# One bias table over the whole score row, transposed probabilities in two PSUM banks, an early query weight, later keys, and the projection's sums on VectorE

## The chip, the cores and the metric

The kernel runs on one core of a Trainium2 chip. A core has five engines, each with its own queue of instructions worked off in order: TensorE (PE, matrix products; its weight loads are listed apart as PEld), VectorE (DVE), ScalarE (ACT), GpSimd (POOL) and SyncE (SP), which here only issues transfers (DMA). SBUF is the core's working memory and PSUM, eight banks of 512 four-byte words on each of 128 partitions, is where PE writes. An engine waits for another, or for a transfer, at a semaphore; while it waits, everything behind in its queue waits too.

The metric is the device time of one execution in microseconds (us). Single executions scatter by about 0.3%.

## The reference

A two-layer trunk for a prompt of 1024 frames and eight sample streams of 16 frames. Layer 0 is RWKV-7 time mixing, layer 1 is banded attention; each is followed by a gated feed-forward part. All numbers are float32. The change lies in the attention of layer 1, which is this (cut to what matters; 16 heads of 64, chunks of 64 frames, eight past chunks):

```python
q_pos = pos0 + start + jnp.arange(qb)
k_pos = pos0 + start - hist_len + jnp.arange(band)
rel = jnp.clip(q_pos[:, None] - k_pos[None, :], -REL_CLIP, REL_CLIP) + REL_CLIP
bias = rel_table[:, rel].astype(jnp.float32)
allowed = ((k_pos[None, :] >= 0) & (k_chunk[None, :] <= q_chunk[:, None])
           & (k_chunk[None, :] >= q_chunk[:, None] - N_PAST_CHUNKS))
s = jnp.einsum('bqhd,bkhd->bhqk', q_b, k_b).astype(jnp.float32) * scale + bias[None]
s = jnp.where(allowed[None, None], s, NEG_INF)
p = jax.nn.softmax(s, axis=-1)
return jnp.einsum('bhqk,bkhd->bqhd', p.astype(v_b.dtype), v_b)
```

The bias depends on the distance of query and key, clipped at 128 frames: over all keys further back it is one constant for each head, and a constant drops out of a softmax. The output is then multiplied by `wb_o` (the projection), gated and added to the stream.

## The kernel before, in words

float32 products are made from two rounded halves (`split`: ACT makes the high half, DVE the difference), three products each.

Attention goes over eight **pairs** of heads (`pair(n)`, L1736), and in a pair over 16 **tiles** (`tile`, L1784): eight blocks of 128 queries for each of the two heads, e = 0 and 1. A tile has up to 640 keys: `nn` near ones (128 or 256), whose bias varies, and `nf` far ones (up to 384), whose bias is the constant. In the eight pairs 64 tiles have 640 keys, 16 have 512, 16 have 384, 16 have 256 and 16 have 128. What the kernel keeps is the negated score, so that the largest score is a minimum.

A tile goes in stages, and `advance` (L1767) interleaves them with those of the tiles before and with other work:

- PE writes the scores into `S` (two banks wide, two buffers). For blocks 4 to 7 an additional matmul of `m1r`, a constant set up at L1638 to L1643, adds 1e30 to the first 64 far keys for the second 64 queries.
- DVE takes the minimum of the far part (`tensor_reduce`, L1809), then one pass over the near part adds the table `bt` and takes the minimum of that and of the far one (L1810; it shows in the profile as a custom instruction and a second one that reads its accumulator).
- ACT takes the exponential with the sum (L1811), DVE normalizes (L1813, L1814).
- PE transposes the probabilities `P` in blocks of 128 into `PT`, a PSUM space of two banks in one buffer (L1819), ACT copies them to `pts` (L1820), and PE multiplies them with the values `vf` into `O`.

The **table** of a head comes from `prep` (L126), which lays the bias values out on the host: 128 queries by 256 keys. At a pair's start `pair` loads it into `bw` (one buffer), DVE subtracts the constant and negates into `bt` (four buffers, L1748), and POOL writes the mask's corner (L1749). `samples` (L1850) does the like for the sample streams with `sbw` and `sbt`, eight small loads a pair; a sample's probabilities, its product with the cached values `vc` and the result's transposition use `PT` too (L1894, the products under the helper's line L139, L1909), and DVE copies the result into `so` (L1913).

Beside the tiles runs a generator, `qgen`: the **queries** for pair n+2 (`queries`, L1722: the weight `wq[n]` is loaded in two halves `h`, split into `wh` and `wl`, and multiplied into `acc`; then a norm, `ht` and `xin`), and in the last two pairs part of the projection. `kprep` and `qprep` load the keys and queries of one head from DRAM into a `slot` and split them (names `h` in the profile). For the even head of the next pair they are called at a pair's start, for the odd one near its end. `kv` (up to L1605) makes keys and values, and the queries of pairs 0 and 1, ahead of the first pair.

`attproj` (L1920) does the rest of the projection for the second half of the frames, and between its steps `strassen_in` (L1280) prepares the feed-forward input: norms, and sums and differences of blocks (L1295), which run on POOL unless another engine is given.

The order on each engine is not written out: a scheduler goes through the program as it is written, with its own idea of durations, and places each instruction in its engine's queue. A buffer's next use waits until all that read its former content have ended; pools of several buffers go round.

Of the kernel before, what the change touches and what calls it, by code (L numbers as in the profile page):

```python
# [9 lines left out]
F32R = mybir.dt.float32r  # L10
# [66 lines left out]
def prep(i):  # L77
    i = {k: np.asarray(v) for k, v in i.items()}
    d = {}
# [43 lines left out]
    d["ck"] = i["cache_k"].reshape(8, 512, 8, 128).transpose(2, 3, 0, 1)  # L123
    d["cv"] = i["cache_v"].reshape(8, 4, 128, 8, 128).transpose(3, 2, 0, 1, 4)
    q, u = np.arange(128)[:, None], np.arange(256)[None, :]
    d["rel"] = i["rel_bias"][0][:, np.minimum(256 + q - u, 256)]  # L126
    for l in range(2):
        d[f"wg{l}"] = _tiles(i["w_gate"][l])
        d[f"wu{l}"] = _tiles(i["w_up"][l])
# [12 lines left out]
class Trunk:  # L142
# [1419 lines left out]
    def kv(self, H, X, end):  # L1562
        nc = self.nc
        kn, qn = (self.cp.tile([128, 1], F32, name=n) for n in ("kn2", "qn2"))
        nc.vector.tensor_scalar(kn, self.P("kn", 0), -0.5, None, ALU.mult)
        nc.vector.tensor_scalar(qn, self.P("qn", 0), 0.5 * 0.125, None, ALU.mult)
        self.qn = qn
        nw = 4
        W = [self.halves(self.a["wk"][n]) for n in range(nw)]
        for c in (1, 0):  # L1570
            for n in range(nw):
                self.head(n, c, W[n], H, kn[:, 0:1], self.kT)
                for _ in range(3):
                    next(end, None)
            for _ in end:
                pass
        for n in range(nw, 8):
            W = self.halves(self.a["wk"][n])
            for c in (1, 0):
                self.head(n, c, W, H, kn[:, 0:1], self.kT)  # L1580
        self.HQ = {}
        Aq = self.gain("nm1", 56)
        for n in range(4):
            W = [h for u in range(2) for h in self.halves(self.a["wv"][n, u])]
            for c in range(2):
                for w in range((4, 5)[c]):
                    ws = slice(w * 128, (w + 1) * 128)
                    pz = self.wide()[:, 0:256]
                    for k in range(8):
                        ks = slice(k % 2 * 256, (k % 2 + 1) * 256)  # L1590
                        wh, wl = W[k // 2]
                        self.mm3(pz, H[c][0][k][:, ws], H[c][1][k][:, ws], wh[:, ks], wl[:, ks], k == 0, k == 7)
                    vt = self.ev("vt")[:, 0:256]
                    nc.scalar.activation(vt, pz, AF.Copy)
                    nc.sync.dma_start(self.o["v"][4 * c + w, :, n * 256:(n + 1) * 256], vt)
                if n == 3:
                    self.HQ[c] = self.feats(c, F32R), self.feats(c, F32R)
                    for _ in self.normed_split(c, *X[c], Aq, 48, *self.HQ[c]):
                        pass
        self.KQ = {}  # L1600
        for e in range(2):
            self.kprep(0, e)
        for n in range(2):
            if n:
                self.evt = lambda tag: self.slot(1)  # L1605
            W = self.halves(self.a["wq"][n])
            for c in range(2):
                self.head(n, c, W, self.HQ, qn[:, 0:1], self.qT)
            if n == 0:
                for e in range(2):  # L1610
                    self.qprep(0, e)
# [18 lines left out]
    def attention(self, ctx):  # L1630
# [4 lines left out]
        self.evt = lambda tag: self.pp.tile([128, 320], F32, tag=tag, name=self.nm(tag), bufs={"xin": 2, "ht": 5}[tag])  # L1635
        self.qbd = at.tile([128, 4, 2, 16], F32, name="qbd")
        nc.gpsimd.memset(self.qbd, 0.0)
        m1 = self.att("pts", [128, 640], 2)[:, 0:192]  # L1638
        self.m1r = at.tile([128, 192], F32R, name="m1r")
        nc.gpsimd.memset(m1, 0.0)  # L1640
        nc.gpsimd.memset(m1[0:1, 64:128], 1.0)
        nc.gpsimd.memset(m1[0:1, 128:192], 1e30)
        nc.scalar.activation(self.m1r, m1, AF.Copy)  # L1643
        self.X, self.xs = {}, {}
        self.O = self.bank("O", 1)
        self.flow = [None] * 3
        for n in range(8):
            if n < 6:
# [73 lines left out]
    def queries(self, n):  # L1722

        nc = self.nc
        W = self.halves(self.a["wq"][n])
        yield
        for c, o, m in ((0, 0, 256), (0, 256, 256), (1, 0, 320), (1, 320, 320)):
            yield from self.head_steps(n, c, o, m, W, self.HQ, self.qn[:, 0:1], self.qT)
# [6 lines left out]

    def pair(self, n):  # L1736
        nc = self.nc
        if n < 7:
            self.kprep(n + 1, 0)
            self.qprep(n + 1, 0)  # L1740
        vf = self.att("vf", [128, 8, 128], 2)
        nc.sync.dma_start(vf, self.o["v"][0:8, :, n * 128:(n + 1) * 128].rearrange("w p d -> p w d"))
        bias = []
        for e in range(2):
            r = self.att("bw", [128, 256], 1)
            nc.sync.dma_start(r, self.a["rel"][2 * n + e])
            bt = self.att("bt", [128, 256], 4)
            nc.vector.tensor_scalar(bt, r, r[:, 0:1], -1.0, ALU.subtract, ALU.mult)  # L1748
            nc.gpsimd.memset(bt[0:64, 192:256], 1e30)  # L1749
            bias.append(bt)  # L1750
        order = [(e, qt) for qt in range(8) for e in range(2)]
        groups = self.samples(n)
        for i, (e, qt) in enumerate(order):
            self.advance(self.tile(n, qt, e, vf, bias[e]))
            if n == 6 and i in (4, 5, 6, 8, 9, 10):
                self.xprep(*divmod((4, 5, 6, 8, 9, 10).index(i), 3))
                if i == (4, 5, 6, 8, 9, 10)[2]:
                    self.qgen = self.proj_part()
            if n == 7 and i in (4, 5):
                self.xprep(i - 4, 3)  # L1760
            if (e, qt) == (0, 7) and n < 7:
                self.kprep(n + 1, 1)
                self.qprep(n + 1, 1)
            if i in (1, 9):
                self.advance(next(groups))
# [16 lines left out]
    def tile(self, n, qt, e, vf, bias):  # L1782
# [7 lines left out]
        h = slice(64 * e, 64 * e + 64)  # L1790
        kq = self.KQ[n, e]

        def score(ps, t0, m, mask=False):
            ks = slice(t0 * 128, t0 * 128 + m)
            mm(nc, ps, kq[0][:, qsl], kq[1][:, ks], True, False)
            if mask:
                mm(nc, ps[:, 0:64], self.m1r[:, 0:128], self.m1r[:, 128:192], False, False)
            mm(nc, ps, kq[0][:, qsl], kq[2][:, ks], False, True)


# [1 line left out]
        P = self.att("P", [128, 640], 3)  # L1802
        S = self.wide_bank("S", 2)
        if nf:
            score(S[:, 512 - nf:512], k0, nf, qt >= 4)
        near = S[:, 512:512 + nn]
        score(near, n0, nn)
        if nf:
            nc.vector.tensor_reduce(st[:, 0:1], S[:, 512 - nf:512], AX.X, ALU.min)  # L1809
        nc.vector.tensor_tensor_reduce(near, near, bias[:, 256 - nn:256], 1.0, st[:, 0:1] if nf else 3.0e38, ALU.add, ALU.min, st[:, 1:2])  # L1810
        nc.scalar.activation(P[:, 0:nf + nn], S[:, 512 - nf:512 + nn], AF.Exp, bias=st[:, 1:2], scale=-1.0, accum_out=st[:, 2:3])  # L1811
        yield
        nc.vector.reciprocal(st[:, 4:5], st[:, 2:3])  # L1813
        nc.vector.tensor_scalar(P[:, 0:nf + nn], P[:, 0:nf + nn], st[:, 4:5], None, ALU.mult)  # L1814
        yield
        pts = self.att("pts", [128, 640], 2)
        pt = self.wide_bank("PT", 1)
        for j in range(nk):
            nc.tensor.transpose(pt[:, j * 128:(j + 1) * 128], P[:, j * 128:(j + 1) * 128], self.C("ident"))  # L1819
        nc.scalar.activation(pts[:, 0:nk * 128], pt[:, 0:nk * 128], AF.Copy)  # L1820
        yield
        if not e:
            self.even = pts
# [11 lines left out]
    def heads_out(self, n, t0, O):  # L1835
# [1 line left out]
        nc = self.nc  # L1837
        w = O.shape[-1]
        if n < 7:
            o = self.att("o", [128, 256], 2)  # L1840
            nc.vector.tensor_copy(o[:, 0:w], O)
            nc.sync.dma_start(self.og[n, :, t0:t0 + w], o[:, 0:w])
            return
# [4 lines left out]
    def samples(self, n):  # L1848
        nc = self.nc
        qs, kn = self.att("qsm", [128, 128]), self.att("ksm", [128, 128])  # L1850
        for t, src in ((qs, self.qT), (kn, self.kT)):
            nc.sync.dma_start(t, src[:, n, 1024:1152])
        r = self.att("sbw", [128, 144], 1)
        for e in range(2):
            for b in range(4):
                nc.sync.dma_start(r[b * 32 + e * 16:b * 32 + e * 16 + 16], self.a["rel"][2 * n + e, 0:16, 0:144])
        bt = self.att("sbt", [128, 144], 1)
        nc.vector.tensor_scalar(bt, r, r[:, 0:1], -1.0, ALU.subtract, ALU.mult)
        so = self.att("so", [128, 8, 16], 2)
        for g in range(2):  # L1860
            yield self.sample_group(n, g, qs, kn, bt, so)
# [1 line left out]
    def sample_group(self, n, g, qs, kn, bt, so):  # L1863
# [25 lines left out]
        nc.vector.reciprocal(st[:, 4:5], st[:, 2:3])  # L1889
        yield  # L1890
        pts = self.att("pts", [128, 640], 2)
        pt = self.wide_bank("PT", 1)
        for j in range(4):
            nc.tensor.transpose(pt[:, j * 128:(j + 1) * 128], P[:, j * 128:(j + 1) * 128], self.C("ident"))  # L1894
        nc.tensor.transpose(pt[0:16, 512:640], P[:, 512:528], self.C("ident"))
        nc.scalar.activation(pts[:, 0:512], pt[:, 0:512], AF.Copy)
        nc.scalar.activation(pts[0:16, 512:640], pt[0:16, 512:640], AF.Copy)
        yield
        O = self.wide_bank("PT", 1)
        quarters = [(b, slice(b * 32, b * 32 + 32)) for b in range(4)]  # L1900
        for j in range(4):
            for b, bs in quarters:
                mm(nc, O[bs, 0:128], pts[:, j * 128 + b * 32:j * 128 + b * 32 + 32], vc[:, b, j], j == 0, False)
        for b, bs in quarters:
            mm(nc, O[bs, 0:128], pts[0:16, 512 + b * 32:512 + b * 32 + 32], vn[:, b], False, True)
        on = self.att("on", [128, 128], 1)
        nc.vector.tensor_scalar(on, O[:, 0:128], st[:, 4:5], None, ALU.mult)
        pt = self.wide_bank("PT", 1)
        nc.tensor.transpose(pt[:, 0:128], on, self.C("ident"))  # L1909
        pv = pt[:, 0:128].rearrange("p (b e t) -> p b e t", b=4, e=2)  # L1910
        for e in range(2):
# [5 lines left out]
    def attproj(self, B, x2, x3, rest):  # L1917
# [5 lines left out]
        A = self.gain("nf1", 80)  # L1923
        r = self.sq_done(next(rest))
        t = [self.slot(1)[:, :1024] for _ in range(4)]
        sub = self.strassen_in(B, x3, r, A, 72, 0, [t[k // 2][:, k % 2 * 512:(k % 2 + 1) * 512] for k in range(8)])
        st = self.sq_open()
        st.acc = self.rs[:, 640:1280]
        for n in range(8):
# [63 lines left out]
```

## Time and profile before

| | |
|---|---|
| runs timed | 3: 3821.11, 3823.53 and 3833.7 us |
| median | 3823.53 us |
| the profiled execution's own time | 3810.6 us |
| its span, first to last instruction | 3808.8 us |
| clock granted to TensorE, mean | 0.944 |
| the attention's pairs, about | 2430 to 2900 us of the span |
| the rest of the projection and the feed-forward input, about | 2900 to 3000 us |

The profile is one execution. In its rows a group has its line, engine, operation, what it writes and reads, its count, then busy us and the mean ns of one, then the idle time of the engine just before with what ended it. Rows of waits have the engine and line that waited, the engine and line that it waited for, us in all, times, and the longest. Rows of a timeline begin with the time of start and the duration in us. PE's matmuls are pipelined, so that the duration of one is longer than the distance between two; busy time over count is nearer to what one costs.

### The profile page before, as it was taken

Reading aid. Unit: us, or ns where it says so; the run is one execution under the profiler, and the core shown is the slowest. Engines: PE = TensorE matmul, PEld = TensorE weight load, DVE = VectorE, ACT = ScalarE, POOL = GpSimd, SP = SyncE. Lnnn points to the kernel's source line nnn. Section 1 sums busy time; section 2 is a strip of 40 time slices with the busy share of each in tenths; the row PEclk is TensorE's granted clock in tenths of the full one; section 3 lists DMA queues with packets and bytes.
Section 4 is the critical chain, followed back from the end, with each engine's and each line's share of the span. In section 5 each row is a group of like instructions: output and inputs, shape, how many; then the busy total and the mean of one; then the engine's idle time right before and its main releaser. Section 6 shows DMA issues by size and latency. Waiting matters only on the chain.

```text
span 3808.8 us, 72340 instructions
## 1 busy us (share of the span) xinstructions
PE 3494.9 (92%) x28614; PEld 3089.7 (81%) x28614; DVE 2282.6 (60%) x4484; ACT 1574.8 (41%) x3007; POOL 589.1 (15%) x516
## 2 busy tenths in 40 slices
PE   5789989989899799999999899789889799999999
PEld 3677778777667699999888879677677699999998
DVE  4666667765445855455456742666675755545667
ACT  5545546554223533333311353565654533333310
POOL 0000000000011154443000100000000245544000
PEclk8887899899699899999999999999999899999999
DMA  5776776676665322224655112454564322222521
GB/s 209 235 221 168 206 221 178 194 211 199 189 193 176 124 81 75 76 74 145 221 177 182 69 67 95 148 157 130 156 202 162 113 87 73 76 75 95 172 86 66
DMA packets 426995, 550.87 MB, mean 145 GB/s; under 512 B 128384, under 2 KB 294784, under 8 KB 422176
## 3 DMA queue, kind: packets, MB, share of 16 engines
q1 hardware_dynamic: 351344, 447.53, 36.9%
q0 software_dynamic: 22224, 80.36, 7.0%
q10 hardware_dynamic: 53088, 18.36, 2.1%
q8 instruction: 225, 3.69, 0.4%
q14 instruction: 114, 0.93, 0.1%
HBM read 412.70 MB, written 133.40 MB: 143 GB/s over the span
## 4 chain that ended last, share of the span: by engine, by line
PE 67%; DMA 12%; DVE 10%; ACT 5%; issue 4%; SPq 1%; ACTq 0%; POOL 0%; DVEq 0%; POOLq 0%
PE S L139 32%; PE PT L139 16%; PE acc L139 10%; PE st L139 3%; PE O L139 2%; PE G L139 1%; PE PT L1819 1%; PE aux L139 1%; DVE h L269 1%; DMA TT<-Z 1%; DVE wlo L269 1%; PE Y L139 1%; ACT pts L1820 1%; DMA raw<-in_rw_o 1%; DMA Z<-T 0%
## 5 line engine op out<-in xcount | busy, mean ns | idle before, releaser
L139 PE MATMUL S<-h,w 128*128 128x320 f32 (+1 forms) x4944 | 684.7, 297 | 11.6 <-ACT h L268 3.6
L139 PEld LDWEIGHTS S<-h,w 128*128 128x128 f32 x4944 | 667.9, 190 | 16.8 <-ACT h L268 4.1
L139 PE MATMUL acc<-mx,whi 128*128 128x384 f32 x1728 | 506.0, 370 | 35.9 <-ACT whi L268 14.0
L139 PE MATMUL S<-h,wh 128*128 128x320 f32 (+1 forms) x2844 | 527.8, 337 | 12.0 <-DVE h L1166 5.8
L139 PEld LDWEIGHTS S<-h,wh 128*128 128x128 f32 x2844 | 454.0, 188 | 68.4 <-issue 11.7
L268 ACT ACTIVATE w<-rq 128x512 fp32r<-128x512 f32 x308 | 192.2, 629 | 503.1 <-PE S L139 195.7
L139 PEld LDWEIGHTS acc<-mx,whi 128*128 128x128 f32 x1728 | 335.6, 203 | 68.3 <-ACT whi L268 18.3
L269 DVE TENSOR_TENSOR w<-rq,w 128x512 fp32r<-128x512 f32 x308 | 266.3, 868 | 204.1 <-ACT w L268 203.5
L139 PE MATMUL PT<-h,w 128*128 128x320 f32 (+1 forms) x2448 | 347.1, 297 | 15.5 <-ACT w L268 8.4
L139 PEld LDWEIGHTS PT<-h,w 128*128 128x128 f32 x2448 | 332.5, 190 | 17.4 <-ACT w L268 8.6
L139 PE MATMUL acc<-mx,wlo 128*128 128x384 f32 x864 | 315.0, 365 | 7.7 <-DVE wlo L269 7.7
L139 PE MATMUL PT<-h,wh 128*128 128x320 f32 (+1 forms) x1428 | 287.3, 344 | 11.6 <-DVE wh L269 3.9
L1365 POOL TENSOR_TENSOR t<-t,t 128x576 f32<-128x576 f32 (+1 forms) x132 | 222.2, 1684 | 428.0 <-ACT t L1372 311.3
L139 PEld LDWEIGHTS PT<-h,wh 128*128 128x128 f32 x1428 | 233.7, 190 | 43.1 <-issue 6.0
L139 PEld LDWEIGHTS acc<-mx,wlo 128*128 128x128 f32 x864 | 173.9, 201 | 20.1 <-DVE wlo L269 12.4
L269 DVE TENSOR_TENSOR wlo<-raw,whi 128x1024 fp32r<-128x1024 f32 x114 | 139.0, 1221 | 82.9 <-ACT whi L268 82.0
L269 DVE TENSOR_TENSOR h<-h,h 128x1024 fp32r<-128x1024 f32 (+4 forms) x112 | 122.9, 1111 | 91.5 <-ACT h L268 74.9
L268 ACT ACTIVATE wh<-rq 128x512 fp32r<-128x512 f32 x124 | 74.8, 626 | 242.5 <-PE S L139 160.0
L268 ACT ACTIVATE h<-h 128x1024 fp32r<-128x1024 f32 (+4 forms) x112 | 103.3, 935 | 172.4 <-DMA h<-sd 112.5
L268 ACT ACTIVATE whi<-raw 128x1024 fp32r<-128x1024 f32 x114 | 119.6, 1052 | 123.3 <-PE acc L139 64.0
L1365 DVE TENSOR_TENSOR t<-S,t 128x576 f32<-128x576 f32 (+1 forms) x116 | 86.3, 744 | 126.0 <-PE S L139 125.9
L1432 DVE TENSOR_TENSOR h<-h,S 128x640 f32<-128x640 f32 (+1 forms) x150 | 111.8, 750 | 78.5 <-PE S L139 78.3
(452 smaller groups left out, 5662.3 us busy)
## 6 DMA issues: line engine op xcount, KB each, us to landing
h<-in_wada SPq DMA_DIRECT2D x64, 512.0 KB, 6.1
rq<-in_wg SPq DMA_DIRECT2D x88, 256.0 KB, 2.6
rq<-in_wu SPq DMA_DIRECT2D x88, 256.0 KB, 2.6
rq<-in_wd SPq DMA_DIRECT2D x88, 256.0 KB, 3.0
raw<-in_wada POOLq DMA_DIRECT2D x32, 512.0 KB, 4.5
kc<-in_ck SPq DMA_DIRECT2D x16, 1024.0 KB, 5.0
vc<-in_cv SPq DMA_DIRECT2D x16, 1024.0 KB, 6.1
sd<-t SPq DMA_DIRECT2D x88, 160.0 KB, 1.9
```

What stands on the lines that cost most here:

```text
L139: return nc.tensor.matmul(out, lhsT, rhs, start=start, stop=stop)
L268: self.nc.scalar.activation(hi, x, AF.Copy)
L269: self.nc.vector.tensor_tensor(lo, x, hi, ALU.subtract)
L1365: eng.tensor_tensor(out, x, y, ALU.add)
L1432: nc.vector.tensor_tensor(y, y, d, ALU.add)
L1819: nc.tensor.transpose(pt[:, j * 128:(j + 1) * 128], P[:, j * 128:(j + 1) * 128], self.C("ident"))
L1820: nc.scalar.activation(pts[:, 0:nk * 128], pt[:, 0:nk * 128], AF.Copy)
```

## The change

Five edits:

1. **The table covers the whole row.** `prep` lays out 641 columns for each query: 384 for far keys (zero, or 1e30 where the mask was), 256 for near ones with the mask's corner in it, and the constant. One pass (now L1813) adds it to all scores of a tile and takes the minimum; the far minimum, the mask's matmuls with `m1r`, and POOL's corner go. The load, 128 by 641 for 128 by 256, goes straight into `bt`, which has three buffers for four and no `bw` ahead of it, and DVE subtracts and negates the near part in place (L1753). The sample's table is loaded into `sbt` likewise.
2. **Two banks.** `PT` becomes one tile for the whole attention. The first three transpositions of a tile go into its first bank and are copied, the others into its second and are copied apart (L1825). The sample's product and its transposition go into the second bank; its intermediate `on` is in an `xin` buffer, and `o` has one buffer for two.
3. **The third query weight** (`wq[2]`) is loaded whole in `kv`, ahead of the second group of queries, and `queries(2)` only splits it.
4. **Pair 1's even keys and queries** are asked for after the fourth tile of pair 0, where they stood at its start.
5. **`attproj`** has `strassen_in` use DVE for its sums.

```diff
-    d["rel"] = i["rel_bias"][0][:, np.minimum(256 + q - u, 256)]
+    near = i["rel_bias"][0][:, np.minimum(256 + q - u, 256)]
+    near[:, 0:64, 192:256] = -1e30
+    far = np.zeros((16, 128, 384), np.float32)
+    far[:, 64:128, 0:64] = 1e30
+    d["rel"] = np.concatenate([far, near, near[:, :, 0:1]], 2)
...
             if n:
+                self.q2 = self.slot(1)[:, :1024]
+                nc.sync.dma_start(self.q2, self.a["wq"][2])
...
-        self.O = self.bank("O", 1)
+        self.O, self.PT = self.bank("O", 1), self.wide_bank("PT", 1)
...
-        W = self.halves(self.a["wq"][n])
+        if n == 2:
+            W = []
+            for p in range(2):
+                W.append([self.wq.tile([128, 512], F32R, tag=t, name=self.nm("wh"), bufs=3) for t in ("wh", "wl")])
+                self.split(*W[p], self.q2[:, p * 512:(p + 1) * 512])
+        else:
+            W = self.halves(self.a["wq"][n])
...
-        if n < 7:
+        if 0 < n < 7:
             self.kprep(n + 1, 0)
             self.qprep(n + 1, 0)
...
-            r = self.att("bw", [128, 256], 1)
-            nc.sync.dma_start(r, self.a["rel"][2 * n + e])
-            bt = self.att("bt", [128, 256], 4)
-            nc.vector.tensor_scalar(bt, r, r[:, 0:1], -1.0, ALU.subtract, ALU.mult)
-            nc.gpsimd.memset(bt[0:64, 192:256], 1e30)
+            bt = self.att("bt", [128, 641], 3)
+            nc.sync.dma_start(bt, self.a["rel"][2 * n + e])
+            nc.vector.tensor_scalar(bt[:, 384:640], bt[:, 384:640], bt[:, 640:641], -1.0, ALU.subtract, ALU.mult)
...
             self.advance(self.tile(n, qt, e, vf, bias[e]))
+            if n == 0 and i == 3:
+                self.kprep(1, 0)
+                self.qprep(1, 0)
...
-            score(S[:, 512 - nf:512], k0, nf, qt >= 4)
-        near = S[:, 512:512 + nn]
-        score(near, n0, nn)
-        if nf:
-            nc.vector.tensor_reduce(st[:, 0:1], S[:, 512 - nf:512], AX.X, ALU.min)
-        nc.vector.tensor_tensor_reduce(near, near, bias[:, 256 - nn:256], 1.0, st[:, 0:1] if nf else 3.0e38, ALU.add, ALU.min, st[:, 1:2])
+            score(S[:, 512 - nf:512], k0, nf)
+        score(S[:, 512:512 + nn], n0, nn)
+        S = S[:, 512 - nf:512 + nn]
+        nc.vector.tensor_tensor_reduce(S, S, bias[:, 640 - nf - nn:640], 1.0, 3.0e38, ALU.add, ALU.min, st[:, 1:2])
...
-        pt = self.wide_bank("PT", 1)
-        for j in range(nk):
-            nc.tensor.transpose(pt[:, j * 128:(j + 1) * 128], P[:, j * 128:(j + 1) * 128], self.C("ident"))
-        nc.scalar.activation(pts[:, 0:nk * 128], pt[:, 0:nk * 128], AF.Copy)
+        for i, m in ((0, min(nk, 3)), (3, nk - 3)):
+            if m > 0:
+                pt = self.PT[:, 512:] if i else self.PT
+                for j in range(i, i + m):
+                    nc.tensor.transpose(pt[:, (j - i) * 128:(j - i + 1) * 128], P[:, j * 128:(j + 1) * 128], self.C("ident"))
+                nc.scalar.activation(pts[:, i * 128:(i + m) * 128], pt[:, 0:m * 128], AF.Copy)
...
-        O = self.wide_bank("PT", 1)
+        O = self.PT[:, 512:]
...
-        sub = self.strassen_in(B, x3, r, A, 72, 0, [t[k // 2][:, k % 2 * 512:(k % 2 + 1) * 512] for k in range(8)])
+        sub = self.strassen_in(B, x3, r, A, 72, 0, [t[k // 2][:, k % 2 * 512:(k % 2 + 1) * 512] for k in range(8)], nc.vector)
```

The instruction queues show what the scheduler makes of it; a row has the line, the operation, what it writes and reads, its size, and the kinds of semaphores it waits for (an engine's name, or a DMAHW one for a transfer).

First DVE, at the end of pair 0. Before, the subtraction of a table of pair 2 from its raw load, with a sample's result copied ahead of it and the norm of some queries behind:

```order
L1810 ISA S_25935,st_25933<-S_25935,bt_25309,st_25933 128x256 [waits DVE_49]
L1810 ISA st_25933 128x1
L1841 COPY o_25827<-so_25362 128x128 [waits DMAHW0_49,DVE_49]
L269 TENSOR_TENSOR h_25966<-h_25974,h_25966 64x1024 [waits DMAHW0_49,Activation_49]
L1748 TENSOR_SCALAR bt_26696<-bw_26694 128x256 [waits DMAHW1_49,DVE_49]
L1813 RECIPROCAL st_25873<-st_25873 128x1 [waits Activation_49]
L329 SCALAR_TENSOR_TENSOR ht_26141<-acc_26140,ht_26141 128x256 [waits Activation_49]
```

With the change, DVE at the same place: the last pass that reads the first head's table `bt_25283` of pair 0, and five rows on the subtraction in `bt_25942`, whose transfer takes over that buffer; then the sample's result `xin_25787`, which PE transposes:

```order
L1813 ISA S_25838,st_25836<-S_25838,bt_25283 128x640 [waits PE_49]
L1813 ISA st_25836 128x1
L273 TENSOR_TENSOR h_25884<-h_25885,h_25883 128x1024 [waits Activation_49]
L1816 RECIPROCAL st_25811<-st_25811 128x1 [waits Activation_49]
L1817 TENSOR_SCALAR P_25812<-P_25812,st_25811 128x640 [waits DVE_49,PE_49]
L1753 TENSOR_SCALAR bt_25942<-bt_25942 128x256 [waits DMAHW4_49]
L1915 TENSOR_SCALAR xin_25787<-PT_25272,st_25651 128x128 [waits PE_49]
L273 TENSOR_TENSOR h_25882<-h_25890,h_25882 64x1024 [waits Activation_49]
L1813 ISA S_25896,st_25894<-S_25896,bt_25286 128x640 [waits PE_49]
```

SP, with the change, at that place: the transfer into `bt_25942` waits for DVE, that is for the pass above, and between it and the transfer for the next table stand the sample's values:

```order
L1626 DMA h_25928<-out_kT 64x1024 [waits DMAHW3_49]
L1752 DMA bt_25942<-in_rel 128x641 [waits DMAHW4_49,DVE_49]
L1876 DMA vc_26017<-in_cv 128x2048 [waits DMAHW5_49,PE_49]
L1874 DMA vn_26015<-out_v 16x4x128 [waits DMAHW6_49,PE_49]
L1752 DMA bt_26614<-in_rel 128x641 [waits DMAHW7_49,DVE_49]
L1847 DMA og<-o_25792 128x128 [waits DMAHW0_49,DVE_49]
```

So the subtraction moved from behind a transfer that had its own buffer to a few rows behind the pass that frees its buffer.

The second place is PE's queue in pair 0 or 1, around a tile's transpositions. Before, all blocks of a tile in one go, after a wait for ACT's copy of the tile ahead:

```order
L1819 MATMUL PT_25945<-cst,P_25874 128x128 [waits Activation_49]
L1819 MATMUL PT_25945<-cst,P_25874 128x128 x4
L139 MATMUL O_25275<-pts_25911,vf_25300 64x128
L139 MATMUL O_25275<-pts_25863,vf_25300 64x128
L139 MATMUL O_25275<-pts_25911,vf_25300 64x128
```

With the change, a tile of 512 keys: three blocks, then the scores of another tile and part of a norm, then the fourth block (`x2` counts repeated rows):

```order
L1824 MATMUL PT_25272<-cst,P_25541 128x128 [waits DVE_49,Activation_49]
L1824 MATMUL PT_25272<-cst,P_25541 128x128 x2
L143 MATMUL S_25684<-h_24981,h_24980 128x384 [waits PE_49,Activation_49]
L143 MATMUL S_25684<-h_24982,h_24980 128x384
L143 MATMUL S_25684<-h_24981,h_24980 128x256
L143 MATMUL S_25684<-h_24982,h_24980 128x256
L143 MATMUL acc_25693<-ht_25694,cst 128x320 [waits Activation_49]
L1824 MATMUL PT_25272<-cst,P_25541 128x128 [waits Activation_49]
L143 MATMUL O_25271<-pts_25600,vf_25281 64x128
```

One wait for ACT became two, and the second is for the copy of the same tile's first three blocks, which read the other bank.

More of the change, by code (lines that the diff above doesn't have):

```diff
@@ L1637, in attention @@
         nc.gpsimd.memset(self.qbd, 0.0)
[L1638 to L1643, printed above, removed]
         self.X, self.xs = {}, {}
-        self.O = self.bank("O", 1)
+        self.O, self.PT = self.bank("O", 1), self.wide_bank("PT", 1)
         self.flow = [None] * 3
@@ L1791, in tile, with score @@
         kq = self.KQ[n, e]
-        def score(ps, t0, m, mask=False):
+        def score(ps, t0, m):
             ks = slice(t0 * 128, t0 * 128 + m)
             mm(nc, ps, kq[0][:, qsl], kq[1][:, ks], True, False)
-            if mask:
-                mm(nc, ps[:, 0:64], self.m1r[:, 0:128], self.m1r[:, 128:192], False, False)
             mm(nc, ps, kq[0][:, qsl], kq[2][:, ks], False, True)
@@ L1804, in tile @@
         if nf:
-            score(S[:, 512 - nf:512], k0, nf, qt >= 4)
-        near = S[:, 512:512 + nn]
-        score(near, n0, nn)
-        if nf:
-            nc.vector.tensor_reduce(st[:, 0:1], S[:, 512 - nf:512], AX.X, ALU.min)
-        nc.vector.tensor_tensor_reduce(near, near, bias[:, 256 - nn:256], 1.0, st[:, 0:1] if nf else 3.0e38, ALU.add, ALU.min, st[:, 1:2])
-        nc.scalar.activation(P[:, 0:nf + nn], S[:, 512 - nf:512 + nn], AF.Exp, bias=st[:, 1:2], scale=-1.0, accum_out=st[:, 2:3])
+            score(S[:, 512 - nf:512], k0, nf)
+        score(S[:, 512:512 + nn], n0, nn)
+        S = S[:, 512 - nf:512 + nn]
+        nc.vector.tensor_tensor_reduce(S, S, bias[:, 640 - nf - nn:640], 1.0, 3.0e38, ALU.add, ALU.min, st[:, 1:2])
+        nc.scalar.activation(P[:, 0:nf + nn], S, AF.Exp, bias=st[:, 1:2], scale=-1.0, accum_out=st[:, 2:3])
         yield
@@ L1839, in heads_out @@
         if n < 7:
-            o = self.att("o", [128, 256], 2)
+            o = self.att("o", [128, 256], 1)
             nc.vector.tensor_copy(o[:, 0:w], O)
@@ L1852, in samples @@
             nc.sync.dma_start(t, src[:, n, 1024:1152])
-        r = self.att("sbw", [128, 144], 1)
+        bt = self.att("sbt", [128, 145], 1)
         for e in range(2):
             for b in range(4):
-                nc.sync.dma_start(r[b * 32 + e * 16:b * 32 + e * 16 + 16], self.a["rel"][2 * n + e, 0:16, 0:144])
-        bt = self.att("sbt", [128, 144], 1)
-        nc.vector.tensor_scalar(bt, r, r[:, 0:1], -1.0, ALU.subtract, ALU.mult)
+                nc.sync.dma_start(bt[b * 32 + e * 16:b * 32 + e * 16 + 16, 1:145], self.a["rel"][2 * n + e, 0:16, 384:528])
+        nc.vector.tensor_copy(bt[:, 0:1], bt[:, 1:2])
+        nc.vector.tensor_scalar(bt[:, 1:145], bt[:, 1:145], bt[:, 0:1], -1.0, ALU.subtract, ALU.mult)
+        bt = bt[:, 1:145]
         so = self.att("so", [128, 8, 16], 2)
@@ L1891, in sample_group @@
         pts = self.att("pts", [128, 640], 2)
[L1892 to L1897, printed above, removed]
+        for i, m in ((0, 3), (3, 1)):
+            pt = self.PT[:, 512:] if i else self.PT
+            for j in range(i, i + m):
+                nc.tensor.transpose(pt[:, (j - i) * 128:(j - i + 1) * 128], P[:, j * 128:(j + 1) * 128], self.C("ident"))
+            if i:
+                nc.tensor.transpose(pt[0:16, 128:256], P[:, 512:528], self.C("ident"))
+                nc.scalar.activation(pts[0:16, 512:640], pt[0:16, 128:256], AF.Copy)
+            nc.scalar.activation(pts[:, i * 128:(i + m) * 128], pt[:, 0:m * 128], AF.Copy)
         yield
-        O = self.wide_bank("PT", 1)
+        O = self.PT[:, 512:]
         quarters = [(b, slice(b * 32, b * 32 + 32)) for b in range(4)]
@@ L1905, in sample_group @@
             mm(nc, O[bs, 0:128], pts[0:16, 512 + b * 32:512 + b * 32 + 32], vn[:, b], False, True)
-        on = self.att("on", [128, 128], 1)
+        on = self.ev("xin")[:, 0:128]
         nc.vector.tensor_scalar(on, O[:, 0:128], st[:, 4:5], None, ALU.mult)
-        pt = self.wide_bank("PT", 1)
+        pt = self.PT[:, 512:]
         nc.tensor.transpose(pt[:, 0:128], on, self.C("ident"))
```

## The prediction

> **What bounds the kernel now.** I read the page's busy shares first, then the same by stage, then the waits of TensorE (PE) inside the attention stage, and last the rows of the groups that the change touches.
>
> ```profile
> PE 3494.9 (92%) x28614; PEld 3089.7 (81%) x28614; DVE 2282.6 (60%) x4484; ACT 1574.8 (41%) x3007; POOL 589.1 (15%) x516
> ```
>
> The long stage of attention, with the columns named in the first row:
>
> ```profile
> core 0: us, PE busy (x) PEld busy (x) DVE busy (x) ACT busy (x) POOL busy (x), PEclk, DMA share, GB/s
> 2460.00:2900.00 440.00, 387.27 (x3471) 314.54 (x3470) 297.03 (x888) 255.87 (x584) 1.88 (x13) 0.97 0.52 160
> ```
>
> PE is the bound, at 92% of the span. The change works between 2420 and 3000 us. In the long stage PE is busy for 387 of 440 us, DVE for 297 and ACT for 256: only PE's 53 us without work, and what PE does itself, can be won there. Who ends PE's waits:
>
> ```profile
> PE PT L1819 <- ACT pts L1820: 21.9, 29, 3.2
> PE PT L1819 <- DVE so L1913: 15.3, 11, 4.4
> PE PT L139 <- ACT pts L1820: 6.3, 6, 1.6
> PE PT L1894 <- ACT pts L1820: 3.1, 7, 0.6
> ```
>
> (Columns: us in all, times, longest.) Almost all are for the PSUM space PT, which holds the transposed probabilities: 31.3 us until ACT has copied them out, 15.3 us until DVE has copied a sample result out of it. One large wait of the first kind, in the timelines of PE and ACT:
>
> ```profile
> 2549.14 0.71 PE L1819 MATMUL PT<-cst,P 128*128 128x128 f32 x5
> 2552.90 1.07 PE L1819 MATMUL PT<-cst,P 128*128 128x128 f32 x5 [3.06 <-ACT pts L1820]
> ```
>
> ```profile
> 2549.90 2.09 ACT L268 ACTIVATE h<-h 128x1024 fp32r<-128x1024 f32 x2 [3.84 <-PE PT L1819]
> 2551.90 0.36 ACT L1514 ACTIVATE xin<-acc 128x256 f32<-128x256 f32 x1
> 2552.17 0.68 ACT L1820 ACTIVATE pts<-PT 128x640 f32<-128x640 f32 x1
> ```
>
> The copy itself is 0.68 us, but ACT came to it 2.3 us late, behind two splits of the next pair's keys. An undisturbed round trip is 0.10 us, the copy, and 0.05 us (2552.85 to 2552.90).
>
> **The two banks: +3 us (-8 to +8).** The copy's rows, with the work that PE can put between two uses of PT:
>
> ```profile
> L1820 ACT ACTIVATE pts<-PT 128x640 f32<-128x640 f32 x58 | 40.5, 698 | 36.0 <-PE PT L1819 29.3 <-PE O L139 6.3
> L1820 ACT ACTIVATE pts<-PT 128x384 f32<-128x384 f32 x16 | 7.8, 490 | 6.1 <-PE PT L1819 6.1
> L1820 ACT ACTIVATE pts<-PT 128x256 f32<-128x256 f32 x15 | 5.6, 376 | 14.0 <-PE PT L1819 13.9
> ```
>
> ```profile
> L139 PE MATMUL O<-pts,vf 128*64 128x128 f32 x876 | 89.9, 293 | 0.0
> L139 PE MATMUL acc<-h,wh 128*128 128x256 f32 x456 | 67.1, 293 | 2.7 <-ACT wh L268 1.9 <-DVE xin L1166 0.5 <-DVE ht L329 0.3
> ```
>
> One copy of 698 ns becomes one of 490 and one of 376: 168 ns more for ACT, 64 times, 11 us of busy time and a little more in the smaller tiles. That would be cheap if PE filled one bank while the other is read. The order of the changed kernel says that it doesn't: each of its 96 two-bank tiles has its fourth transposition wait for the copy of its own first three, and the next tile's first wait for the copy of the second bank. PT is one tile, and it is guarded as one. So 141 round trips become 238, shorter ones. I went through PE's queue in both orders and set each trip (0.15 us and the copy) against the matmuls that stand between, at busy time over count (O 103 ns, acc 147, and each other group by its own row). Before, 49 trips are short of work, by 29.9 us in all (the trace's own 31.3 says that the count is fair); after, 83 are, by 32.5. Hence +3. It is -8 if the shorter copies are passed by the splits less often, and +8 if 97 more trips meet ACT's queue as the trip of 2552.17 did, four times at 2 us. The 15.3 us for the sample's result stay: all 16 of those waits stand in the new order too, on a bank that the waiting transpositions don't write.
>
> By the Trainium skill (PSUM — Partial Sum Buffer, "Summary: rules for kernel authors") PSUM may be read while matmuls run if they write another bank. By that rule this term would be a gain; no run here shows it yet, and the order's waits are stricter than the rule.
>
> **The bias table: -5 us on what it removes.** Far and near scores now get one pass:
>
> ```profile
> L1809 DVE TENSOR_REDUCE st<-S 128x1 f32<-128x384 f32 x61 | 33.8, 555 | 11.4 <-PE S L139 10.8
> L1810 DVE CUSTOM_DVE_ANT_0 S<-S,bt,st 128x256 f32<-128x256 f32 x91 | 44.4, 490 | 1.9
> L1810 DVE CUSTOM_DVE_ANT_0 S<-S,bt 128x256 f32<-128x256 f32 x14 | 6.0, 429 | 0.2
> L1810 DVE CUSTOM_DVE_ANT_0 S<-S,bt 128x128 f32<-128x128 f32 x14 | 4.0, 298 | 0.6 <-PE S L139 0.5
> ```
>
> 128 columns cost 131 ns, so 640 are estimated at 429 + 3 x 131 = 0.82 us, in place of 555 + 490 ns: 0.22 us less, 64 times, and by the same slope about as much on the 32 tiles with a narrower far part: some 21 us of DVE time. DVE isn't the bound; I put -2 (0 to -4) on the path, through the 15.3 us that PE waits for DVE's queue. The far mask's matmul goes 64 times:
>
> ```profile
> 2466.42 0.44 PE L139 MATMUL S<-h,h 128*128 128x384 f32 x1
> 2466.70 0.19 PE L139 MATMUL S<-m1r 128*128 128x64 f32 x1
> 2466.72 0.65 PE L139 MATMUL S<-h,h 128*128 128x384 f32 x3
> ```
>
> Its 0.19 us is pipeline depth: the next matmul begins 0.02 us after it. Between 0.02 and 0.19 us each I take 0.05, near the lower end, since starts are what count: -3 us (-1 to -12).
>
> **The table's load: +18 us (0 to +38), the term that decides.** The raw table had its own buffer and the negated one four; now the load writes the table itself, 328 KB for 128, in three buffers. The order shows what that does at each of the seven pair boundaries: a load waits for the last pass that reads the old table, and its own subtraction stands 4 to 10 rows behind that pass on DVE. DVE works in order, so it stands still until the load has landed, and behind it stand the sample's result and the norm that PE waits for. This happens 13 times.
>
> ```profile
> L1748 DVE TENSOR_SCALAR bt<-bw 128x256 f32<-128x256 f32 x13 | 4.6, 352 | 3.8 <-DMA bw<-in_rel 3.4
> ```
>
> ```profile
> DMA to landing us min/median/max: 2.0/3.4/9.7
> ```
>
> ```profile
> h<-out_kT SPq DMA_DIRECT2D x24, 256.0 KB, 5.1
> ...
> vf<-out_v SPq DMA_DIRECT2D x6, 512.0 KB, 3.9
> ```
>
> (The second row is the old table's load.) Before, DVE lost 3.8 us in all to these loads. After: pass 0.82, its second instruction and the issue some 0.4, landing 4.2 (between the old table's 3.4 and the 5.1 of the 256 KB loads), subtraction 0.35, the next instruction as much, together 6.1 us from the end of a score matmul to the first matmul that waits behind. The PE work between, counted in the new order as above: 2.1 us at four places, 2.4 at three, 2.6 at two, 3.2 at one, 6.0 at two and 6.7 at one. The shortfalls add up to 4 x 4.0 + 3 x 3.7 + 2 x 3.5 + 2.9 + 0.2 = 37 us. PE already loses time at these places: about half of the 15.3 us, and three ACT waits like the one above (some 3 us each, 3.2 the longest), some 17 us, that lie beside the new ones; 20 remain, of which I count 18, as a late PE finds the later copies done. With landing at 2.0 us the shortfall is 16 and all of it is covered: 0. With none covered: about 38.
>
> By the Trainium skill (DMA: Bandwidth & Descriptors, "Anatomy of one DMA — SWDGE (gpsimd) path") a transfer takes 2.0 us and 1 us per 436 KB: an estimate of 2.8 us here, and the sum below would come to about zero. The old table's 128 KB (2.3 us by that) took 3.4 in the median, so the trace doesn't agree.
>
> **The third query weight and the later keys: -2 us (0 to -5).**
>
> ```profile
> PE acc L139 <- ACT wh L268: 8.8, 1, 8.8
> ```
>
> ```profile
> 2433.96 1.06 ACT L268 ACTIVATE h<-h 128x1024 fp32r<-128x1024 f32 x1 [5.61 <-DMA h<-out_kT]
> ```
>
> PE's 8.8 us end with the weight's split, which stood on ACT behind the split of pair 1's keys, whose load landed at 2433.9. The weight now lands early, but in the new order the keys' load is still issued at once (its buffer is free) and their split still stands ahead of the weight's. Only what is behind is less crowded, so -2; -5 would take the two splits changing places.
>
> **Projection's sums: -4 us (-2 to -5).**
>
> ```profile
> PE PT L139 <- DVE wh L269: 3.9, 1, 3.9
> ```
>
> ```profile
> L1295 POOL TENSOR_TENSOR h<-h,h 128x256 f32<-128x256 f32 x12 | 12.2, 1041 | 173.5 <-DMA vf<-in_wo 173.5
> ```
>
> ```profile
> 2977.81 7.04 DVE L269 TENSOR_TENSOR h<-h,h 128x256 fp32r<-128x256 f32 x8
> 2986.23 0.74 DVE L269 TENSOR_TENSOR h<-h,h 128x256 fp32r<-128x256 f32 x2
> ```
>
> 16 sums of 1.04 us run one after the other on POOL, and DVE's rows beside them take 0.88 us each where 0.37 is usual. On DVE 16 sums cost about 6 us and the stretching goes, 4 us: DVE is no later, and PE's wait of 3.9 us behind them goes, with a small one ahead of it.
>
> **The sum.** +3 - 2 - 3 + 18 - 2 - 4 = +10 us on the profiled execution's 3810.6, or 3821. The runs' median is 3823.53, 12.9 us above that execution, so the forecast on its scale is 3833.5: slower by 0.26%, at the edge of what a measurement of this kernel tells from no change (about 0.3%, 11.5 us).
>
> **Rivals.**
> 1. *Tables land late (slower).* Between a boundary's two table loads SP issues the sample's values, 1 MB; the old table took up to 9.7 us in such company. Each us of landing beyond 4.2 costs about 10 us, as ten of the 13 places are short. From 4.4 us up the kernel is slower by over 0.3%; at 6 us it is 3851. Against it: the old median of 3.4.
> 2. *Tables land in time.* At 3 us the term is 6 and the sum about -2: 3821. For it: the minimum of 2.0, and half of the loads under 3.4 at 128 KB.
> 3. *The banks do overlap in effect.* If shorter copies meet PE only once it has other work, most of the 31.3 us goes except three waits behind splits (9 us): -20 in place of +3, the sum -13, 3810.5. For it: 155 of 238 trips have work enough. Against it: so had 92 of 141, with the waits seen. The skill's rule on banks, above, points here.
> 4. *The change doesn't do what it says.* Of the five edits, the order already denies it to two (the banks, the later keys); this is in the sum.
>
> **Chances.** The forecast 0.48 (+1 to +20 by the bounds of its terms: half within 0.3%, half slower), rival 1 0.19 (slower), rival 2 0.15 (within 0.09, faster 0.06), rival 3 0.18 (faster 0.16, within 0.02). Together: faster by over 0.3% 0.22, within 0.36, slower 0.42. The range leaves out the far ends of rivals 1 and 3: 3807 to 3858.
>
> **What would show it.** DVE idle ahead of the subtraction in place, ended by the table's load, 13 times and 25 us or more in all: the deciding term. If it is under 10 us, rival 2. PE's waits for PT from ACT near 30 us or above: the banks are in series; under 12, rival 3. The mask's 64 matmuls gone with PE's starts only 3 us closer. PE's 8.8 us wait at the start still over 6. No POOL row in the projection, and PE's wait of 3.9 us there gone. The forecast is wrong if PE hardly waits behind those subtractions, or if waits elsewhere grow, as on ACT's copies.

## The result, and the profile after

The changed kernel is **slower by 1.09%**: 3862.52 us in the median of six runs, against 3822.32 for six of the kernel before; the ratio is 1.0109, with a 95% interval of 1.0088 to 1.013. The forecast was 3833.5, from 3807 to 3858: the side was right, the size was a quarter of it, and the time lies 4.5 us above the range. The profiled execution is the slowest of the six (3868.62 us, span 3866.8).

The stage from the first transposition of probabilities to the last, by the busy time of each engine, first before, then after:

```profile
2441.00:2933.00 492.00, 432.10 (x3854) 350.72 (x3853) 328.18 (x969) 278.21 (x636) 2.17 (x15) 0.97 0.53 164
```

```profile
2446.00:3000.00 554.00, 467.38 (x3810) 352.76 (x3811) 314.70 (x877) 286.74 (x731) 0.00 (x0) 0.94 0.49 153
```

(Columns as in the prediction: length, busy us of PE, PEld, DVE, ACT and POOL, PE's granted clock, DMA.) The stage is 62 us longer. PE's idle time, length less busy, went from 60 to 87 us; but its *busy* time grew by 35 us too, with the mask's matmuls gone. Its waits in the long stretch (2460 to 2900 us of the changed kernel's span):

```profile
PE PT L1824 <- ACT pts L1825: 26.1, 35, 2.9
PE PT L1824 <- DVE so L1921: 11.6, 12, 2.5
PE acc L143 <- DVE ht L333: 7.2, 7, 2.2
PE PT L1824 <- ACT pts L1905: 6.7, 13, 0.5
PE PT L1917 <- DVE xin L1915: 4.4, 5, 1.0
...
PE PT L143 <- ACT pts L1825: 3.6, 5, 0.7
PE O L143 <- DVE o L1846: 3.3, 1, 3.3
```

Then the transpositions and the products with the values in the same stretch, before (the products' row is in the prediction) and after:

```profile
L1819 PE MATMUL PT<-cst,P 128*128 128x128 f32 x446 | 73.1, 285 | 37.3 <-ACT pts L1820 21.9 <-DVE so L1913 15.3
```

```profile
L143 PE MATMUL O<-pts,vf 128*64 128x128 f32 x778 | 91.3, 310 | 3.3 <-DVE o L1846 3.3
L1824 PE MATMUL PT<-cst,P 128*128 128x128 f32 x391 | 81.3, 304 | 45.4 <-ACT pts L1825 26.1 <-DVE so L1921 11.6 <-ACT pts L1905 6.7
```

By busy time over count a transposition now stands at 208 ns for 164, a product at 117 for 103, but that does not make them dearer. A matmul counts as busy until its result is out, some 0.28 us after its start, and so the end of each run of like matmuls is counted to the group although the next group has begun. The runs have become shorter: before, five transpositions in one run took 0.71 us (a row of the prediction); now they come as three and two:

```profile
2617.21 0.55 PE L1824 MATMUL PT<-cst,P 128*128 128x128 f32 x3
2618.74 0.38 PE L1824 MATMUL PT<-cst,P 128*128 128x128 f32 x2
```

Within a run the transpositions start 0.11 us apart in both traces. What the longer busy time is made of is worked out below, from the run that has the two-bank edit alone. One part is PE's clock, which fell to half more often:

```profile
2466.00:2473.00 7.00, 5.68 (x23) 4.36 (x23) 4.10 (x12) 3.97 (x11) 0.00 (x0) 0.54 0.27 102
```

This stretch has a 2.3 us wait for ACT in it (PE starts again at 2467.32), and 23 matmuls in 7 us. In the profile's record of the granted clock this stage has 12 such episodes of 3.4 or 6.8 us at half clock, 30.7 us lost if PE had work throughout; before there were 6, and 13.7 us.

On DVE: its wait for the table's load, the load's time to landing, and the pass over 640 columns.

```profile
DVE bt L1753 <- DMA bt<-in_rel: 10.8, 9, 3.8
```

```profile
bt<-in_rel SPq DMA_DIRECT2D x16, 320.5 KB, 3.4
```

```profile
L1813 DVE CUSTOM_DVE_ANT_0 S<-S,bt 128x640 f32<-128x640 f32 x64 | 53.1, 830 | 26.8 <-PE S L143 24.7
```

The table's load stopped DVE nine times, for 10.8 us and not the 25 or more foretold, since 320 KB landed as fast (3.4 us in the median) as 128 KB had. The full-width pass takes 830 ns, as estimated (0.82).

### The profile page after: what moved, and what is told of

It is laid out like the page before. It is cut to its first block, busy times and chain, and to the rows that moved or that the text cites. A ratio compares the mean times of both kernels' runs of the same rounds, so it can differ in the third digit from the quotient of the medians.

```text
span 3866.8 us, 72265 instructions
## 1 busy us (share of the span) xinstructions
PE 3535.0 (91%) x28550; PEld 3094.8 (80%) x28550; DVE 2268.8 (59%) x4412; ACT 1580.9 (41%) x3102; POOL 575.4 (15%) x481
## 4 chain that ended last, share of the span: by engine, by line
PE 67%; DMA 13%; DVE 10%; issue 5%; ACT 4%; SPq 1%; ACTq 0%; POOL 0%; DVEq 0%; POOLq 0%
PE S L143 31%; PE PT L143 15%; PE acc L143 11%; PE st L143 3%; PE O L143 2%; DMA raw<-in_rw_o 1%; PE PT L1824 1%; PE aux L143 1%; DMA TT<-Z 1%; DVE h L273 1%; PE G L143 1%; DMA Z<-T 1%; DMA kc<-in_ck 1%; PE Y L143 1%; DVE wlo L273 1%
## 5 line engine op out<-in xcount | busy, mean ns | idle before, releaser
L143 PE MATMUL S<-h,w 128*128 128x320 f32 (+1 forms) x4944 | 690.3, 299 | 11.6 <-ACT h L272 3.8
L143 PEld LDWEIGHTS S<-h,wh 128*128 128x128 f32 x2844 | 455.0, 189 | 69.2 <-issue 11.6
```

The source lines that it names most:

```text
L143: return nc.tensor.matmul(out, lhsT, rhs, start=start, stop=stop)
```

## The experiments

Two theories stood against each other. A: the loss is the two-bank edit, because PT is guarded as one tile and each two-bank tile makes two round trips to ACT in series. B: it is the load of the table that DVE waits for. Ratios are to the kernel before.

**The two-bank edit undone in the changed kernel**

```diff
-        for i, m in ((0, min(nk, 3)), (3, nk - 3)):
...
+        pt = self.wide_bank("PT", 1)
+        for j in range(nk):
+            nc.tensor.transpose(pt[:, j * 128:(j + 1) * 128], P[:, j * 128:(j + 1) * 128], self.C("ident"))
+        nc.scalar.activation(pts[:, 0:nk * 128], pt[:, 0:nk * 128], AF.Copy)
```

> The changed kernel with the two-bank edit undone: PT is again a buffer per use, a tile's blocks are transposed together and copied once; the other four edits stay. Theory A (the banks: PT is guarded as one tile, so each two-bank tile has two round trips to ScalarE instead of one): the loss of about 40 us against before goes nearly whole, 3815 to 3832 us. Theory B (the table's load on VectorE is the loss): the time stays near the changed kernel's, 3845 to 3865 us.

3808.66 us, ratio 0.9972 (0.9953 to 0.9991): on A's side, and better than its range. The other four edits together are worth 0.3%; the two-bank edit takes that and 1.1% more.

**The two-bank edit alone, on the kernel before**

```diff
+        for i, m in ((0, min(nk, 3)), (3, nk - 3)):
+            if m > 0:
+                pt = self.PT[:, 512:] if i else self.PT
...
+                nc.scalar.activation(pts[:, i * 128:(i + m) * 128], pt[:, 0:m * 128], AF.Copy)
```

> The kernel before with the two-bank edit of tiles and samples alone. Theory A: 25 to 45 us slower than before, 3847 to 3867 us, with TensorE's waits for ScalarE's copies up in number from about 45 to about 85. Theory B: within 8 us of before, 3815 to 3830 us.

3873.43 us, 1.0141 (1.0113 to 1.0168), 53 us: beyond A's range, and B is out. 0.9972 times 1.0141 is 1.0113, against the changed kernel's own 1.0109, so the parts add up. A's count of waits missed: in the stage PE's transpositions and the sample's products wait for the copies 51 times for 44, not 85. Its stage:

```profile
2457.00:3007.00 550.00, 481.47 (x3885) 369.12 (x3886) 333.18 (x968) 286.98 (x732) 2.19 (x15) 0.93 0.48 148
```

Of 58 us more than before, only 9 are idle time of PE (68.5 for 59.9); PE is busy for 49 us longer, at a clock of 0.93 for 0.97. The trace says roughly of what. This is an estimate: each distance from one matmul's start to the next was set against the usual distance of two such matmuls at full clock with no wait. Some 24 us more lie in stretches at half clock (half of them is 38 us, for 14). Some 8 are starts that stand behind a semaphore and come late, by too little to show as idle time. Some 10 are the shorter runs: at full clock it is 0.20 us from the start of a run's last transposition or product to the start of a product or transposition behind it, against 0.11 us from one transposition to the next or from one pair of products to the next, and the products come in 166 runs for 127. The other 7 are elsewhere, most of them matmuls of the projection that now fall into the stage.

**The banks as two tiles, in the changed kernel, and the control**

```diff
-                pt = self.PT[:, 512:] if i else self.PT
+                pt = self.bank(("PT", "PU")[i > 0], 1)
...
+                psx.close()
+                self.ps, self.two = mk("psE"), True
```

> The changed kernel with its two banks as two tiles of one bank each, guarded apart, so that TensorE can fill one while ScalarE reads the other; for this the PSUM pool is closed and opened again around the attention. Theory A: all of the loss goes and some of the waits of before with it, 3800 to 3825 us. Theory B: 3845 to 3865 us. If separate guards help no more than one copy does, it comes out as that one within 6 us.

3803.05 us, 0.9946 (0.9927 to 0.9965): the loss is gone. It is within 6 us of the run with one copy, and the intervals overlap, so this run doesn't show that two banks apart beat one copy. The PSUM pool had to be closed and opened around the attention for this, which the control has too, with PT left as one tile:

> The changed kernel with nothing but the PSUM pool closed and opened again around the attention; PT stays one tile. If the gain of the banks apart comes from the guards: as the changed kernel, 3852 to 3872 us. If it comes from the pool: below 3840 us.

3873.33 us, 1.013 (1.0106 to 1.0155): as the changed kernel, 1 us beyond the range given. So what helps is the guard, with the order that the scheduler makes of it, and not the pool.

**The banks as two tiles, on the kernel before**

> The kernel before with a tile's blocks in two banks that are two tiles, guarded apart, and nothing else of the change (the PSUM pool is closed and opened again around the attention). If separate guards pay for themselves: 5 to 15 us faster, 3806 to 3816 us. If two copies take back what the overlap gives, as the run with two copies in one trip suggests (17 us): within 5 us of before.

3793.19 us, 0.9923 (0.9909 to 0.9938), better than foretold, and here clear of noise. Two banks that can overlap are worth 27 us; PE is idle for 34 us of this stage (the row of its busy times), where it was 60:

```profile
2443.00:2908.00 465.00, 431.35 (x3823) 339.90 (x3823) 320.36 (x963) 281.65 (x730) 2.17 (x15) 0.97 0.54 168
```

```profile
L1830 PE MATMUL PT<-cst,P 128*128 128x128 f32 x312 | 56.9, 285 | 10.2 <-ACT pts L1831 10.2
L1830 PE MATMUL PU<-cst,P 128*128 128x128 f32 x137 | 31.1, 301 | 13.4 <-ACT pts L1831 9.8 <-DVE so L1926 3.6
```

By busy time over count its transpositions stand at 196 ns (88.0 us over 449), nearly as in the changed kernel, in a kernel that is faster than before: that number tells of the cut runs and not of the loss.

**Two copies, but one round trip, on the kernel before**

```diff
-        nc.scalar.activation(pts[:, 0:nk * 128], pt[:, 0:nk * 128], AF.Copy)
+        for j0, j1 in ((0, min(nk, 3)), (3, nk)):
+            if j1 > j0:
+                nc.scalar.activation(pts[:, j0 * 128:j1 * 128], pt[:, j0 * 128:j1 * 128], AF.Copy)
```

> The kernel before with only the copy of a tile's transposed blocks cut in two (three blocks, then the rest), after all five transpositions as before: ScalarE has the changed kernel's longer copies, TensorE still waits once for each tile. If the loss of the two-bank edit is the second round trip, with what TensorE loses around each wait: within 12 us of before, 3812 to 3834 us. If it is ScalarE's additional 11 to 16 us of copying: 15 us slower or more, 3836 us or above.

3838.9 us, 1.0046 (1.0029 to 1.0063): by the median on the side of the copies, which I had not thought likelier. But the ten runs fall into two groups, five from 3830 to 3833 us and five from 3845 to 3851: 10 or 28 us above before, one in the range of the second trip and one in that of the copies. Taken by the median, some 17 of the 53 us come with two copies alone and 36 with the second trip; the groups leave that division open. Nor is it ACT's time alone that changes: the products now start with the first copy, and wait for ACT 23 times where the transpositions did. Here (the profile is of the faster group) PE is idle for no longer than before, 58 us of the stage by the row of busy times:

```profile
2441.00:2953.00 512.00, 453.74 (x3846) 359.02 (x3845) 324.69 (x966) 282.13 (x714) 3.03 (x15) 0.94 0.52 158
```

but the clock is 0.94 for 0.97, with 30.7 us lost to half clock for 13.7: most of the 20 us by which the stage is longer.

**The table without its load wait, in the changed kernel**

```diff
-            bt = self.att("bt", [128, 641], 3)
-            nc.sync.dma_start(bt, self.a["rel"][2 * n + e])
-            nc.vector.tensor_scalar(bt[:, 384:640], bt[:, 384:640], bt[:, 640:641], -1.0, ALU.subtract, ALU.mult)
+            r = self.att("bw", [128, 257], 2)
+            nc.sync.dma_start(r, self.a["rel"][2 * n + e][:, 384:641])
+            bt = self.bt[e]
+            nc.vector.tensor_scalar(bt[:, 384:640], r[:, 0:256], r[:, 256:257], -1.0, ALU.subtract, ALU.mult)
```

> The changed kernel, but the table's near part is loaded into a raw buffer of its own (two of them) and VectorE subtracts from there into two lasting tables of 640 columns, so that no subtraction waits for a load that waits for a pass. Theory A: 3852 to 3865 us, at most 10 us better than the changed kernel. Theory B: 3825 to 3846 us, 16 us better or more. In either case VectorE's waits for the table's load (10.8 us in the changed kernel) go below 3 us.

3861.28 us, 1.0097 (1.0064 to 1.0129): the changed kernel's time within what can be told. DVE's wait for the table's load is nearly gone (its row of waits):

```profile
DVE bt L1757 <- DMA bw<-in_rel: 1.4, 1, 1.4
```

The stage of the profiled execution is 10.8 us shorter (542.5 for 553.3). Together with the banks apart:

> Banks guarded apart and the table without the load wait, both together, the other edits of the change kept. If the table's wait costs the 16 us or more that the forecast gave it once the banks don't cover it: 3780 to 3792 us. If it is nearly free on the path, as it was in the changed kernel: 3796 to 3806 us, no different from the banks apart alone.

3792.97 us, 0.993 (0.9904 to 0.9956), against 0.9946 with banks apart alone: the intervals overlap, and the stage is 11.7 us shorter (466.2 for 477.9). Both point to some 10 us, but two executions with the same attention differ by 6 us in this stage (last section), and the totals don't settle it.

**Each other part alone, on the kernel before**

> The kernel before with the projection's sums on VectorE alone. The forecast's term: 2 to 5 us faster in the projection, 3816 to 3822 us, not to be told from before by the total; in the trace TensorE's wait of 3.9 us there is gone. The rival, that VectorE now is late there: that wait stays or grows, and the part from the last transposition to the end is no shorter than 876 us.

3817.67 us, 0.9988 (0.9974 to 1.0002), with PE's wait of 3.9 us there gone and the part behind the last transposition at 871.4 us for 876.7. That fits the forecast's -4, but isn't told from nothing: the interval holds 1, and in the run with one copy, which has this edit too, the same part took 876.7 us as before.

> The kernel before with one pass over the whole row, no mask matmuls and two lasting tables (raw loads ahead of them, no load wait); the banks, the weight, the keys and the projection as before. By the forecast's terms: 5 us faster (2 for VectorE, 3 for the mask), 3810 to 3820 us. If the mask's matmuls cost TensorE more than their distance to the next matmul, as the distances between matmuls in the changed kernel say (8 us): 3800 to 3812 us.

3818.45 us, 0.9995 (0.9981 to 1.0009): no gain that can be told. The ratio says 2 us; the interval reaches to 7, so that the forecast's 5 is not excluded, and 8 is.

> The kernel before with the early third weight and the later keys and queries of pair 1 alone. The forecast's term is 0 to 5 us faster, 3816 to 3822 us, with TensorE's wait of 8.8 us at the start still over 6 us, as the keys' load and split are scheduled ahead all the same. If the edit does what it says, that wait falls under 3 us and the time to about 3814 us.

3821.76 us, 1.0011 (0.9997 to 1.0025): no gain. PE's wait for the weight's split at the start, in its row of waits, hardly moves:

```profile
PE acc L139 <- ACT wh L268: 7.6, 2, 7.2
```

**The version that beats both**

```diff
-                pt = self.PT[:, 512:] if i else self.PT
+                pt = self.bank("PT", 2)
```

> As the run with banks apart and the table fixed, but the two banks are two slots that every half tile takes in turn, rather than first blocks always in the one and the others in the other. If waiting for a certain bank costs something: 3782 to 3790 us. If the scheduler's order decides: 3788 to 3800 us, the same as that run within 8 us.

3779.77 us, 0.9893 (0.9866 to 0.992): 40 us faster than before, 83 faster than the changed kernel, and under both ranges. It has all five edits, with the banks as two slots taken in turn and the table from a raw buffer.

```profile
2440.00:2896.00 456.00, 421.27 (x3753) 333.59 (x3753) 299.41 (x869) 280.57 (x729) 0.00 (x0) 0.97 0.57 172
```

```profile
PE PT L1837 <- ACT pts L1838: 13.0, 13, 2.2
```

Above, the stage by busy time, and then PE's waits for ACT's copies, 13 us in 13 times; those for a sample's result are all but gone. Whether taking the slots in turn helps by itself isn't shown: the interval overlaps that of the run with fixed banks and the table fixed (0.9904 to 0.9956).

## Why the prediction was wrong

- **The two banks, +3 us: this step failed.** Measured alone they cost 53 us. That they are in series, as the order showed, was right: in the trace of the changed kernel no tile's transpositions, first or second part, start before the copy ahead of them has ended. What failed is the price: each trip was set against the PE work between, and only a shortfall counted. That sum (32.5 us) is close to what PE's idle time shows for those waits (26.1 + 6.7 + 3.6 us), so the idle time was sized about right, and it is the small part. The count left out what else comes with the second trip: by the estimate above, half clock around the stalls (some 24 us more), starts that come late within a matmul's pipeline (8) and shorter runs (10).
- **The table's load, +18 us: the wait was right, the size too high.** Nine of the 13 waits came, for 10.8 us on DVE. The landing was 3.4 us, not 4.2. What PE waited behind them is less than described: for a sample's result in `so` 11.6 us, and 7.5 without the load wait; for `o` 3.3 us, which goes too; but the norm's 7.2 us stay (7.6) without the load wait, and 5.3 are there with the two banks alone, so they aren't the load's. DVE also waits 4.1 us for the sample's table, now loaded in place, 0.5 before, which the forecast didn't count. The stage shortens by 11 us without the load wait; by the total it can't be told.
- **The table's pass and mask, -5:** 2 us by the ratio, not told from nothing nor from 5.
- **Weight and keys, -2:** nothing, for the reason given: the keys' load and split stay ahead. The wait is 7.2 us in the run with this edit alone and 6.7 in the changed kernel.
- **The projection, -4:** the wait went as described; the size fits, but isn't told from nothing.
- **The rivals.** None happened. Rival 1 had the right side by the wrong mechanism, and so had the forecast: that it came out on the slower side is luck, as its deciding term was the table's load, and without the two banks the kernel is faster (0.9972); rival 3, banks that overlap, is what happens once they are guarded apart, and it then pays 27 us, near the size it was given (-20 in place of +3). (Its chances add up to 0.35 within and 0.43 slower, for the 0.36 and 0.42 given.)
- *Open:* how the 53 us divide between idle time, the clock, late starts and shorter runs is an estimate from single traces. The clock's part was read, not isolated; no run kept PE's clock up through the same waits.

## What to carry to other kernels

A buffer cut in two is two buffers only if it is guarded as two: look in the instruction order for a wait between the halves of one item. Price a further round trip on an in-order engine by more than the idle time that it shows: late starts that stay hidden, shorter runs and a clock that falls around a stall were the larger share here. Don't read a group's busy time over count as the price of one when its runs have changed length. Undo the suspected edit and make it alone: here the two ratios multiply to the whole, which settles which edit it is.

## What the runs showed of the hardware

PE's granted clock fell to 0.50 for 3.4 or 6.8 us around stalls that were mostly shorter: in the kernel before each of its six episodes in this stage begins within 2 us of a wait of 1.2 to 4.4 us. Of the 14 waits of over 1 us there, eight, the longest of 2.6 us, brought none. The Trainium skill (TensorE: Matmul & The Clock Gate, "Part 1") describes such a gate, half clock after about 3.4 us of idling and full again after about 3.4 us of work. The durations agree, though every stretch of this record but the last, at full clock too, is a multiple of 3.41 us; the idle time does not agree, as waits of a microsecond or two can be enough here. The clock also goes with scatter: the run with only the projection changed has the attention of before, and its stage took 6.1 us longer (496.8 for 490.7) with 6.8 us more lost to half clock.

The Trainium skill's rule that one PSUM bank may be read while a matmul writes another (PSUM — Partial Sum Buffer, "Summary: rules for kernel authors") holds here: with the banks apart on the kernel before, transpositions started in one bank during 47 of the 208 copies out of the other, PE's idle time in the stage went from 60 to 34 us, and the time fell by 0.77%.

A load of 320 KB landed in the same 3.4 us in the median as one of 128 KB.
